# Expert layer kernel on one core: 102 up projections beside the gate matrix, and the sparse tile routed first

## The chip, the cores and the metric

The kernel runs on one core of a Trainium2 chip. The metric is the device time of one execution in microseconds; a version's time is the median of several runs. TensorE (PE in the rows), VectorE (DVE), ScalarE (ACT) and GpSimd (POOL) each run their own instruction queue in order; SyncE (SP) issues the plain DMAs, POOL the gathers.

## The reference, cut to what matters

512 tokens of width 1024 pass one layer: attention and convolution, an output projection, then a retrieval over 16384 single-neuron experts (PEER), then an embedding gate. The part that the change touches is the retrieval:

```
q = (mf @ wq).reshape(T, 8, 2, 128)
s = einsum('thcd,cnd->thcn', q, keys)              # 128 keys per half
sv, si = top_k(s, 16)
cand = sv[:, :, 0, :, None] + sv[:, :, 1, None, :]
cs, ci = top_k(cand.reshape(T, 8, 256), 16)
e1, e2 = si of half 0 and of half 1, picked by ci // 16 and ci % 16
experts = (e1 * 128 + e2).reshape(T, 128);  gates = softmax(cs)
a = einsum('cd,ckd->ck', x, u_tab[experts])
h = gelu(a) * gates
y = einsum('ck,ckd->cd', h, v_tab[experts])
```

Each token uses 128 of the 16384 experts. All data is float32.

## The kernel before

The retrieval is done in two ways. The first three token tiles (128 tokens each, NA = 3, TA = 384 tokens) are done **densely**: all 128 chunks c of 128 experts get an up projection (`up(c)`: expert rows by 384 tokens, then Gelu), the result is multiplied by a gate matrix that is zero where a token did not choose an expert, and a down projection (`down_prep(c)`, `down(c)`) adds up into six PSUM banks `y`. The fourth tile is done **sparsely**: `sparse(i)` gathers one expert row per token with an indirect DMA on POOL (256 gathers of 128 rows, first of u, then of v) and reduces it on DVE with one scalar_tensor_tensor (`scr` on L722 for u, `acc` on L730 for v). Four `row` buffers are in use in turn.

Every float32 product is made of three fp32r matmuls (`mm3`, L66 to L68): a weight tile `raw` is copied to a rounded `hi` on ACT and the rest `lo` is subtracted on DVE or POOL. So one up projection is 24 matmuls of 384 columns, one ACT copy (L583), one subtraction (`ulo`, L584) and one Gelu (L594, or L590 if the result goes to DRAM). One down chunk is 18 matmuls of 512 columns (L709).

The stages, in program order:

1. Front: attention, convolution, output projection, second norm. The change leaves it alone.
2. Routing, L596 to L616: 16 query projections of 24 matmuls (`qhi`, `qlo`), 16 times eight key matmul instructions (L611), and `top16` on DVE for each of 16 (head, half) scores of the three dense tiles. The scores of the sparse tile are copied to `sB` by ACT (L612). `pairs` then forms 112 candidate sums per head (L508, L510) and takes their top 16.
3. Gate matrix, L619 to L662: 12 up projections first; then per dense tile a `decodeA` (which expert, which gate) and 16 groups of GB = 8 tokens. A group builds one-hot rows in float16 on DVE (`o1v`, `eq`, and the two products L651 and L652; in every fourth group `o1a` comes from ACT instead of `o1v`), PE multiplies them (16 matmuls of 128 columns, L658) and ACT copies PSUM to `stage` (L660). A full stage (2 MB) goes to `g_spill` in DRAM. One up projection is emitted before every second group.
4. The up projections that are left of `first` (40 in all: chunks 0 to 23 are kept in SBUF, 16 more go to DRAM as `a_spill`), then `routeB` for the sparse tile (16 `top16`, `pairs`, `decode`, and `bidx`, the gather indices).
5. Experts, loop over c = 0 to 127: the up projection of chunk 24 + c or the load of a spilled one, the gate block `gt` for four chunks, the splits of the v tile, 18 down matmuls, and as many `sparse` steps as `sched(c)` asks for. Chunks from 104 on have no up projection.
6. Tail: gate and final norm, output.

The program is written in an order, but a planner at build time puts the instructions of each engine into their final order: it takes what is ready by priority, and up projections are seen to run well ahead of their place in the text. `keep_in_program_order` holds a single instruction back from that. Waits on buffers (two `uhi`, two `ulo`, three `uraw`, two PSUM banks `ups`, six `rbank`, two `stage`) set how far things can run ahead.

Of the kernel before, what the change touches and what calls it, by code (L numbers as in the profile page):

```python
# [10 lines left out]
F32 = mybir.dt.float32  # L11
# [17 lines left out]
NA = 3  # L29
TA = NA * 128  # L30
AHEAD = 24
SPILL = 16
GT = 32
NG = TA // GT
GB = 8
# [3 lines left out]
RATE, LATE = 1.38, 12  # L39
EVERY = 3  # L40
FIRST, STEP = 12, 2
# [12 lines left out]
def hymba_layer(ctx: ExitStack, tc: tile.TileContext, I, out):  # L54
# [38 lines left out]
    # ---------------------------------------------------------------- front  # L93
# [18 lines left out]
    # the tensor engine's clock comes up, and the first table, while the first loads are on their way  # L112
# [51 lines left out]
    # 1 / rms of every token, as a column per token tile and along the free axis of all partitions  # L164
# [78 lines left out]
    # attention in units of (head, query tile), three stages apart  # L243
# [65 lines left out]
    # the layer's own embedding, projected  # L309
# [51 lines left out]
    # the depthwise taps  # L361
# [5 lines left out]
    # conv layer norm + swish  # L367
# [18 lines left out]
    # ------------------------------------------------- output projection, second norm  # L386
    hd = tc.dram_tile([NT, 128, D], F32, name="h1_spill")
    ad = tc.dram_tile([SPILL, 128, TA], F32, name="a_spill")
# [73 lines left out]
    # ------------------------------------------------- expert routing  # L462
# [6 lines left out]
    gap = tc.alloc_tile_pool(name="gap", bufs=AHEAD, reuse_waits="tile")  # L469
# [12 lines left out]
    sB = rbp.tile([128, NH, 2, NK], F32, name="sB")  # L482
    jrep = rbp.tile([128, TOPK, 128], F16, name="jrep")
    A.activation(jrep, iota[:, 0:TOPK, None].to_broadcast([128, TOPK, 128]), AF.Copy)
    ne1 = rt.tile([128, NA, 128], F32, name="ne1")
# [5 lines left out]
    A.activation(irep, iota[:, :, None].to_broadcast([128, 128, 2]), AF.Copy)  # L491

# [8 lines left out]
    # of the sorted pairs (i, j) only those with (i + 1) * (j + 1) <= 16 can be among the first 16:  # L501
    # rows 0..3 whole and the first 4 of the others hold them all, in the order of their index
    NC0, NCAND = 4 * TOPK, 4 * TOPK + 12 * 4

    def pairs(st, t, h):
        sv, si, cs, ci = st
        cand = rbp.tile([128, NCAND], F32, name="cand", bufs=2)
        V.tensor_tensor(cand[:, 0:NC0].rearrange("p (a b) -> p a b", a=4), sv[:, t, h, 0, 0:4][:, :, None].to_broadcast([128, 4, TOPK]),  # L508
                        sv[:, t, h, 1][:, None, :].to_broadcast([128, 4, TOPK]), op=OP.add)
        V.tensor_tensor(cand[:, NC0:].rearrange("p (a b) -> p a b", a=12), sv[:, t, h, 0, 4:TOPK][:, :, None].to_broadcast([128, 12, 4]),  # L510
                        sv[:, t, h, 1, 0:4][:, None, :].to_broadcast([128, 12, 4]), op=OP.add)
        top16(cand, cs[:, t, h], ci[:, t, h], NCAND)
# [40 lines left out]
    def decodeA(t):  # L553
# [4 lines left out]
        A.activation(ne1[:, t], tp[:, 0:128], AF.Copy, scale=-1.0)  # L558
# [17 lines left out]
    first = list(range(AHEAD)) + list(spilled)  # L576

    def up(c):
# [5 lines left out]
        (P if c in first else V).tensor_tensor(lo, raw, f32(hi), op=OP.subtract)  # L584
# [11 lines left out]
    for h in range(NH):  # L596
        for c in range(2):
# [14 lines left out]
            A.activation(sB[:, h, c], sp[:, NA * 128:], AF.Copy)  # L612
            for t in range(NA):
                top16(sp[:, t * 128:t * 128 + 128], setA[0][:, t, h, c], setA[1][:, t, h, c], 128)
        for t in range(NA):
            pairs(setA, t, h)  # L616
    wqp.release()
    gst = tc.alloc_tile_pool(name="gst", bufs=2, reuse_waits="tile")
    for c in first[:FIRST]:  # L619
        up(c)  # L620
    nu = FIRST
    for t in range(NA):
        decodeA(t)
        for b in range(128 // GT):
            stage = gst.tile([128, NK, GT], F32, name="stage")
            for g in range(GT // GB):
                tk = b * GT + g * GB
                if g % STEP == 0 and nu < len(first):
                    up(first[nu])
                    nu += 1  # L630
# [6 lines left out]
                if g % ACT_EVERY == ACT_EVERY - 1:  # L637
                    ab = gst.tile([128, GB, 128], F16, name="ab", bufs=1)
                    for j in range(GB):
                        A.activation(ab[:, j], iota, AF.Abs, bias=ne1[:, t, tk + j:tk + j + 1])  # L640
                    o1 = gst.tile([128, GB, 128], F16, name="o1a", bufs=1)
                    A.activation(o1, ab, AF.Relu, bias=ones[:, 0:1], scale=-1.0)
                    pick1 = [o1[:, j] for j in range(GB)]
                else:
                    o1 = gst.tile(sh, F16, name="o1v")
                    V.tensor_tensor(o1, it, pairwise(e1T), op=OP.is_equal)
                    pick1 = [o1[:, j // 2, :, j % 2] for j in range(GB)]
# [22 lines left out]
    def ahead(c):  # L670
        if c in spilled:
# [241 lines left out]
```

## Time and profile before

| what | us |
|---|---|
| median of 3 runs | 1630.68 (1629.73 to 1630.71) |
| span of the profiled execution | 1628.7 |
| PE busy | 1538.4 (94%) |
| DVE busy | 1296.2 (80%) |
| ACT busy | 706.2 (43%) |
| POOL busy | 537.4 (33%) |

A PE row's duration contains the run through the array, and neighbouring matmuls overlap; so the cost of a matmul is read as the distance between the starts of matmuls that follow each other without a wait. A window of the trace lists the busy time of each engine, the granted TensorE clock as a share of 2.4 GHz, and the share of the DMA engines' time. The profiled execution's span is 2.0 us under the median of the runs.

### The profile page before, as it was taken

How to read it: one execution, taken by the hardware profiler on the slowest of the kernel's cores; microseconds unless marked ns; L12 is line 12 of the kernel's file. 1: busy time of each engine (PE TensorE's matmuls, PEld its weight loads, DVE VectorE, ACT ScalarE, POOL GpSimd, SP SyncE). 2: the span in 40 equal slices, each digit the busy share in tenths (PEclk: the TensorE clock that was granted, in tenths of full speed). 3: DMA queues.
4: the chain of work that ended last, by engine and by line, in shares of the span. 5: the costliest groups of instructions: out<-in, count | busy, mean ns of one | idle time of the engine just before them, and what ended most of it. 6: DMA issues, size and time to landing. Idle time of an engine off the chain costs nothing. (4 is left out here: it accounts for less than half of the span.)

```text
span 1628.7 us, 22295 instructions
## 1 busy us (share of the span) xinstructions
PE 1538.4 (94%) x7945; PEld 1334.0 (82%) x7945; DVE 1296.2 (80%) x2564; ACT 706.2 (43%) x1116; POOL 537.4 (33%) x360
## 2 busy tenths in 40 slices
PE   8999898999688887999999999999999999999997
PEld 6866576888577776988888889999999999997886
DVE  4999875988989998478887888777777777777657
ACT  5434643322488796433333333333333333324432
POOL 1000103442353342244444444444444444430000
PEclk9999998999899998999999999999999999999999
DMA  7210254221234645989999999988988899977612
GB/s 241 93 66 33 74 188 154 93 85 40 78 148 169 241 179 227 316 302 355 330 351 319 347 336 351 328 325 315 330 319 319 325 320 334 328 256 258 211 44 78
DMA packets 147648, 374.83 MB, mean 230 GB/s; under 512 B 12113, under 2 KB 66129, under 8 KB 146001
## 3 DMA queue, kind: packets, MB, share of 16 engines
q1 hardware_dynamic: 110672, 239.18, 42.3%
q0 software_dynamic: 36864, 134.23, 21.9%
q8 instruction: 62, 1.02, 0.2%
q14 instruction: 50, 0.40, 0.1%
HBM read 338.76 MB, written 34.60 MB: 229 GB/s over the span
## 5 line engine op out<-in xcount | busy, mean ns | idle before, releaser
L66 PE MATMUL ups<-mTH,uhi 128*128 128x384 f32 x1024 | 354.9, 347 | 4.0 <-ACT ga L594 4.0
L68 PE MATMUL ups<-mTH,ulo 128*128 128x384 f32 x1024 | 352.9, 345 | 5.6 <-POOL ulo L584 5.6
L67 PE MATMUL ups<-mTL,uhi 128*128 128x384 f32 x1024 | 351.2, 343 | 0.0
L583 ACT ACTIVATE uhi<-uraw 128x1024 fp32r<-128x1024 f32 x128 | 135.6, 1061 | 278.6 <-PE ups L67 251.5
L718 POOL DMA_INDIRECT row<-in_u,bidx x128 | 180.1, 1407 | 224.2 <-DVE scr L722 211.4
L718 POOL DMA_INDIRECT row<-in_v,bidx x128 | 182.6, 1427 | 206.8 <-DVE acc L730 189.4
L709 PE MATMUL y<-vlo,hH 128*128 128x512 f32 x768 | 238.5, 392 | 2.0 <-DVE vlo L63 2.0
L709 PE MATMUL y<-vhi,hH 128*128 128x512 f32 x768 | 239.0, 392 | 0.3 <-ACT vhi L62 0.3
L709 PE MATMUL y<-vhi,hL 128*128 128x512 f32 x768 | 239.0, 392 | 0.0
L66 PEld LDWEIGHTS ups<-mTH,uhi 128*128 128x128 f32 x1024 | 196.6, 192 | 8.6 <-ACT ga L594 4.6
L68 PEld LDWEIGHTS ups<-mTH,ulo 128*128 128x128 f32 x1024 | 196.1, 192 | 7.0 <-POOL ulo L584 6.9
L67 PEld LDWEIGHTS ups<-mTL,uhi 128*128 128x128 f32 x1024 | 196.0, 191 | 4.9
L62 ACT ACTIVATE hH<-hf 128x384 fp32r<-128x384 f32 x128 | 67.0, 524 | 285.2 <-issue 219.3
L63 DVE TENSOR_TENSOR hL<-hf,hH 128x384 fp32r<-128x384 f32 x128 | 71.2, 557 | 146.0 <-ACT hH L62 145.8
L584 POOL TENSOR_TENSOR ulo<-uraw,uhi 128x1024 fp32r<-128x1024 f32 x40 | 123.4, 3090 | 177.3 <-ACT uhi L583 155.6
L709 PEld LDWEIGHTS y<-vlo,hH 128*128 128x128 f32 x768 | 144.0, 188 | 35.4 <-DVE vlo L63 4.0
L709 PEld LDWEIGHTS y<-vhi,hL 128*128 128x128 f32 x768 | 144.2, 188 | 31.3 <-DVE rsq L73 0.2
L722 DVE SCALAR_TENSOR_TENSOR scr<-row,mB 128x1024 f32<-128x1024 f32 x128 | 156.1, 1220 | 15.4 <-DMA row<-in_u,bidx 15.4
L709 PEld LDWEIGHTS y<-vhi,hH 128*128 128x128 f32 x768 | 143.1, 188 | 25.4 <-ACT vhi L62 1.0
L730 DVE SCALAR_TENSOR_TENSOR acc<-row,bh,acc 128x1024 f32<-128x1024 f32 x127 | 162.5, 1279 | 0.0
L63 DVE TENSOR_TENSOR vlo<-vraw,vhi 128x1024 fp32r<-128x1024 f32 x128 | 156.1, 1220 | 0.8 <-ACT vhi L62 0.8
L584 DVE TENSOR_TENSOR ulo<-uraw,uhi 128x1024 fp32r<-128x1024 f32 x88 | 107.5, 1221 | 37.2 <-ACT uhi L583 37.1
(277 smaller groups left out, 2447.9 us busy)
## 6 DMA issues: line engine op xcount, KB each, us to landing
uraw<-in_ut SPq DMA_DIRECT2D x128, 512.0 KB, 6.1
vraw<-in_v SPq DMA_DIRECT2D x128, 512.0 KB, 4.7
g_spill<-stage SPq DMA_DIRECT2D x12, 2048.0 KB, 6.9
gt<-g_spill SPq DMA_DIRECT2D x32, 768.0 KB, 9.7
qraw<-in_wq SPq DMA_DIRECT2D x16, 512.0 KB, 3.6
wraw<-in_w_in SPq DMA_DIRECT2D x15, 512.0 KB, 3.9
woraw<-in_w_out SPq DMA_DIRECT2D x8, 512.0 KB, 4.2
et<-in_wg SPq DMA_DIRECT2D x8, 512.0 KB, 4.3
```

Source lines behind the costliest of these rows:

```text
L62: A.activation(hi, src, AF.Copy)
L63: V.tensor_tensor(lo, src, f32(hi), op=OP.subtract)
L66: T.matmul(ps, wh, xh, start=first, stop=False)
L67: T.matmul(ps, wh, xl, start=False, stop=False)
L68: T.matmul(ps, wl, xh, start=False, stop=last)
L583: A.activation(hi, raw, AF.Copy)
L584: (P if c in first else V).tensor_tensor(lo, raw, f32(hi), op=OP.subtract)
L709: T.matmul(y[t][n], w[:, sl], x[:, n * 512:n * 512 + 512], start=c == 0 and w is hH and x is hi, stop=c == NK - 1 and l)
L718: P.indirect_dma_start(out=row, out_offset=None, in_=I["u"] if i < 128 else I["v"], in_offset=bass.IndirectOffsetOnAxis(ap=bidx[:, j:j + 1 ...
L722: tc.keep_in_program_order(V.scalar_tensor_tensor(scr, row, 1.0, mB, op0=OP.mult, op1=OP.mult, accum_out=ba[:, j:j + 1]))
L730: tc.keep_in_program_order(V.scalar_tensor_tensor(acc, row, bh[:, j:j + 1], acc, op0=OP.mult, op1=OP.add))
```

## The change

- `AHEAD`, `SPILL` and the rest are replaced: 102 of 128 up projections (chunks 0 to 7, kept in SBUF, and 94 others that go to DRAM as `a_spill` and come back in the expert loop) are emitted in the routing and gate stages: 20 before the gate matrix, 4 after each `decodeA`, 3 before each group. The 26 chunks of `DIRECT` (11, 15, ..., 111) are done in the expert loop. The `lo` part of the first 20 is made on POOL, all others on DVE.
- The sparse tile is routed first: its `top16` reads PSUM (no `sB` copy), `routeB` is emitted ahead of the gate stage, and its u gathers are emitted there: two at three places per tile and ROWS = 4 per group, so 114 of the 128 in that stage. The other 14 and the 128 of v stay in the expert loop, spread by a new `sched`.
- `pairs` takes four heads at once (two additions for four heads instead of eight), and for the dense tiles it is emitted with the tile's decode.
- A group has GB = 16 tokens. Every third group's `o1` is made by a POOL subtraction and two ACT instructions over the whole group. The gate matmuls write PSUM with a step of four floats, so that the copy to `stage` reads in order and writes runs of four floats.
- `gt` is loaded for eight chunks at a time.

```
-AHEAD = 24
-SPILL = 16
+KEEP = 8
+DIRECT = [c for c in range(8, 112) if c % 4 == 3]
+GC = 8
-GB = 8
+GB = 16
+HG = 4
-RATE, LATE = 1.38, 12
-EVERY = 3
-FIRST, STEP = 12, 2
+FIRST, PER = 20, 3
+ROWS = 4
...
     def pairs(st, t, h):
         sv, si, cs, ci = st
-        cand = rbp.tile([128, NCAND], F32, name="cand", bufs=2)
...
+        hs = slice(h, h + HG)
+        cand = rbp.tile([128, HG, NCAND], F32, name="cand")
...
+        for j in range(HG):
+            top16(cand[:, j], cs[:, t, h + j], ci[:, t, h + j], NCAND)
...
     def routeB():
-        for h in range(NH):
-            for c in range(2):
-                top16(sB[:, h, c], setB[0][:, 0, h, c], setB[1][:, 0, h, c], 128)
-            pairs(setB, 0, h)
         ef = decode(setB, 0)
         V.tensor_copy(bgate, ef[:, 2])
-        V.scalar_tensor_tensor(ef[:, 0], ef[:, 0], float(NK), ef[:, 1], op0=OP.mult, op1=OP.add)
-        return ef[:, 0]
+        V.scalar_tensor_tensor(bidx, ef[:, 0], float(NK), ef[:, 1], op0=OP.mult, op1=OP.add)
...
-    spilled = {AHEAD + EVERY * i + EVERY - 1: i for i in range(SPILL)}
-    first = list(range(AHEAD)) + list(spilled)
+    spilled = {c: i for i, c in enumerate(c for c in range(KEEP, NK) if c not in DIRECT)}
+    first = list(range(KEEP)) + list(spilled)
+    EARLY = len(first)
...
-        (P if c in first else V).tensor_tensor(lo, raw, f32(hi), op=OP.subtract)
+        (P if c in first[:FIRST] else V).tensor_tensor(lo, raw, f32(hi), op=OP.subtract)
...
-            A.activation(sB[:, h, c], sp[:, NA * 128:], AF.Copy)
+            top16(sp[:, NA * 128:], setB[0][:, 0, h, c], setB[1][:, 0, h, c], 128)
             for t in range(NA):
                 top16(sp[:, t * 128:t * 128 + 128], setA[0][:, t, h, c], setA[1][:, t, h, c], 128)
-        for t in range(NA):
-            pairs(setA, t, h)
+        if h % HG == HG - 1:
+            pairs(setB, 0, h + 1 - HG)
...
-    for c in first[:FIRST]:
-        up(c)
-    nu = FIRST
+    nu, nxt = 0, 0
+
+    def more(n):
+        nonlocal nu
+        while n > 0 and nu < EARLY:
+            up(first[nu])
+            nu += 1
+            n -= 1
+
+    def rows(n):
+        nonlocal nxt
+        while n > 0 and nxt < 128:
+            sparse(nxt)
+            nxt += 1
+            n -= 1
+
+    routeB()
+    more(FIRST)
     for t in range(NA):
+        for h in range(0, NH, HG):
+            pairs(setA, t, h)
+            rows(2)
         decodeA(t)
+        rows(2)
+        more(4)
         for b in range(128 // GT):
             stage = gst.tile([128, NK, GT], F32, name="stage")
             for g in range(GT // GB):
                 tk = b * GT + g * GB
-                if g % STEP == 0 and nu < len(first):
-                    up(first[nu])
-                    nu += 1
+                more(PER)
+                rows(ROWS)
...
-                if g % ACT_EVERY == ACT_EVERY - 1:
-                    ab = gst.tile([128, GB, 128], F16, name="ab", bufs=1)
-                    for j in range(GB):
-                        A.activation(ab[:, j], iota, AF.Abs, bias=ne1[:, t, tk + j:tk + j + 1])
-                    o1 = gst.tile([128, GB, 128], F16, name="o1a", bufs=1)
-                    A.activation(o1, ab, AF.Relu, bias=ones[:, 0:1], scale=-1.0)
+                if (tk // GB + t * (128 // GB)) % ACT_EVERY == ACT_EVERY - 1:
+                    o1 = gst.tile([128, GB, 128], F16, name="o1", bufs=2)
+                    P.tensor_tensor(o1, iota16[:, None, :].to_broadcast([128, GB, 128]),
+                                    e1T[:, t, tk:tk + GB][:, :, None].to_broadcast([128, GB, 128]), op=OP.subtract)
+                    A.activation(o1, o1, AF.Abs)
+                    A.activation(o1, o1, AF.Relu, bias=ones[:, 0:1], scale=-1.0)
...
-                            T.matmul(gb[:, j * 128:j * 128 + 128], o2[:, i, jj // 2, :, jj % 2], pick1[jj], start=i == 0, stop=i == 1)
+                            T.matmul(gb[:, j::4], o2[:, i, jj // 2, :, jj % 2], pick1[jj], start=i == 0, stop=i == 1)
...
-                    A.activation(stage[:, :, t0:t0 + 4].rearrange("p e t -> p t e"),
-                                 gb.rearrange("p (t e) -> p t e", t=4), AF.Copy, scale=1.0 / GS)
+                    A.activation(stage[:, :, t0:t0 + 4], gb.rearrange("p (e t) -> p e t", t=4), AF.Copy, scale=1.0 / GS)
...
-    for c in first[nu:]:
-        up(c)
-    eB = routeB()
...
+    more(EARLY)
+    NU = NK - 24
+    nxt0 = nxt
+    def weight(c):
+        return c + 1 + sum(n <= c + KEEP for n in DIRECT)
     def sched(c):
-        return RATE * (c + 1 + sum(n not in spilled for n in range(AHEAD, AHEAD + min(c + 1, NU)))) - LATE
+        return nxt0 + (256 - nxt0) * weight(c) / weight(NU + 10)
...
     for c in range(NK):
-        if c < NU:
-            ahead(AHEAD + c)
+        if KEEP + c in DIRECT:
+            up(KEEP + c)
+        elif KEEP + c < NK:
+            ga[KEEP + c] = gap.tile([128, TA], F32, name="ga")
+            load(ga[KEEP + c], ad[spilled[KEEP + c]])
         parts = down_prep(c)
```

## Rows read from the trace of the kernel before

**Rows 1.** The page's 40 slices of the span: busy tenths of PE and DVE.
```profile
PE   8999898999688887999999999999999999999997
...
DVE  4999875988989998478887888777777777777657
```

**Rows 2.** Windows: stretch, its length; busy us of each engine, clock, DMA share, GB/s.
```profile
264.00:410.00 146.00, 144.91 (x733) 124.51 (x731) 119.59 (x688) 46.49 (x72) 56.54 (x24) 0.99 0.24 81
410.00:450.00 40.00, 25.96 (x135) 23.98 (x136) 39.58 (x81) 17.65 (x35) 13.70 (x6) 0.83 0.23 79
450.00:646.00 196.00, 157.35 (x1293) 144.34 (x1292) 186.33 (x371) 161.19 (x246) 81.52 (x23) 0.91 0.50 192
646.00:669.00 23.00, 23.00 (x123) 23.00 (x121) 6.83 (x12) 10.06 (x14) 7.06 (x4) 0.91 0.71 260
264.00:669.00 405.00, 351.22 (x2277) 315.83 (x2276) 352.33 (x1149) 235.40 (x364) 158.83 (x56) 0.93 0.39 145
...
669.00:1470.00 801.00, 801.00 (x3978) 722.95 (x3977) 625.79 (x788) 283.61 (x386) 360.49 (x254) 1.00 0.91 327
```

**Rows 3.** Tile hH: count, ns min/median/max, first and last start, us.
```profile
L709 PE MATMUL y<-vhi,hH x768: 387/389/628, 669.1 to 1570.1; 128*128 128x512 f32 x192
```

**Rows 4.** Timeline of PE from 494.7: start us, us, what, count.
```profile
494.71 0.34 PE L67 MATMUL ups<-mTL,uhi 128*128 128x384 f32 x1
...
496.62 2.01 PE L658 MATMUL rbank<-o1v,o 128*128 128x128 f16 x32
498.44 0.42 PE L66 MATMUL ups<-mTH,uhi 128*128 128x384 f32 x1
```

**Rows 5.** Timeline of PE among down projections, two matmuls a row.
```profile
1477.54 0.62 PE L709 MATMUL y<-vhi,hH 128*128 128x512 f32 x2
...
1482.07 0.62 PE L709 MATMUL y<-vlo,hH 128*128 128x512 f32 x2
```

**Rows 6.** Timeline of PE, the key matmuls of one query projection.
```profile
273.20 1.16 PE L611 MATMUL rbank<-keysT,qT 128*128 128x128 f32 x8
```

**Rows 7.** Groups by line: count, busy us, mean ns, idle before and releaser.
```profile
L718 POOL DMA_INDIRECT row<-in_u,bidx x128 | 180.1, 1407 | 224.2 <-DVE scr L722 211.4 <-DMA vraw<-in_v 6.3 <-DVE ulo L584 2.9
...
L722 DVE SCALAR_TENSOR_TENSOR scr<-row,mB 128x1024 f32<-128x1024 f32 x128 | 156.1, 1220 | 15.4 <-DMA row<-in_u,bidx 15.4
...
L583 ACT ACTIVATE uhi<-uraw 128x1024 fp32r<-128x1024 f32 x128 | 135.6, 1061 | 278.6 <-PE ups L67 251.5 <-POOL ulo L584 11.7 <-issue 8.9
...
L584 DVE TENSOR_TENSOR ulo<-uraw,uhi 128x1024 fp32r<-128x1024 f32 x88 | 107.5, 1221 | 37.2 <-ACT uhi L583 37.1
...
L651 DVE TENSOR_TENSOR o<-eq,gTH 128x1024 f16<-128x1024 f16 x48 | 44.8, 933 | 2.2 <-PE rbank L658 2.2
...
L652 DVE TENSOR_TENSOR o<-eq,gTL 128x1024 f16<-128x1024 f16 x48 | 39.3, 819 | 0.0
...
L510 DVE TENSOR_TENSOR cand<-sv 128x48 f32<-128x48 f32 x32 | 22.1, 692 | 0.0
...
L722 DVE DVE_READ_ACCUMULATOR scr<-row,mB 128x1 f32 x128 | 10.6, 83 | 0.0
```

**Rows 8.** Single lines: ns min/median/max, first and last start.
```profile
L651 DVE TENSOR_TENSOR o<-eq,gTH x48: 667/682/2872, 443.6 to 643.1; 128x1024 f16<-128x1024 f16 x48
...
L584 POOL TENSOR_TENSOR ulo<-uraw,uhi x40: 2351/2460/9224, 267.4 to 657.6; 128x1024 fp32r<-128x1024 f32 x40
```

**Rows 9.** Waits from 410 to 650: who for whom, us, times, longest.
```profile
PEld L658 <- DVE o L651: 41.6, 21, 10.1
```

**Rows 10.** Timeline of SP after the last gate group.
```profile
647.44 0.32 SPq L59 DMA_DIRECT2D g_spill<-stage  x1
...
658.42 0.37 SPq L59 DMA_DIRECT2D gt<-g_spill  x1
```

**Rows 11.** Tile row: time of its transfers from issue to landing.
```profile
DMA to landing us min/median/max: 2.0/7.2/11.7
```

**Rows 12.** Waits of SP's queue over the span: us, times, longest.
```profile
SPq L59 <- DVE hf L701: 36.6, 25, 5.2
```

More of the change, by code (lines that the diff above doesn't have):

```diff
@@ L491, in hymba_layer @@
     A.activation(irep, iota[:, :, None].to_broadcast([128, 128, 2]), AF.Copy)
+    iota16 = rt.tile([128, 128], F16, name="iota16")
+    A.activation(iota16, iota, AF.Copy)
     def top16(src, vals, idx, n):
@@ L564, in routeB, with new_row, sparse @@
     def routeB():
-        for h in range(NH):
-            for c in range(2):
-                top16(sB[:, h, c], setB[0][:, 0, h, c], setB[1][:, 0, h, c], 128)
-            pairs(setB, 0, h)
         ef = decode(setB, 0)
         V.tensor_copy(bgate, ef[:, 2])
-        V.scalar_tensor_tensor(ef[:, 0], ef[:, 0], float(NK), ef[:, 1], op0=OP.mult, op1=OP.add)
-        return ef[:, 0]
+        V.scalar_tensor_tensor(bidx, ef[:, 0], float(NK), ef[:, 1], op0=OP.mult, op1=OP.add)
+    def new_row():
+        return gp.tile([128, D], F32, name="row", bufs=4)
+    def sparse(i):
+        j = i % 128
+        row = new_row()
+        P.indirect_dma_start(out=row, out_offset=None, in_=I["u"] if i < 128 else I["v"],
+                             in_offset=bass.IndirectOffsetOnAxis(ap=bidx[:, j:j + 1], axis=0))
+        if i < 128:
+            scr = gp.tile([128, D], F32, name="scr")
+            tc.keep_in_program_order(V.scalar_tensor_tensor(scr, row, 1.0, mB, op0=OP.mult, op1=OP.mult, accum_out=ba[:, j:j + 1]))
+            if j % 32 == 31:
+                js = slice(j - 31, j + 1)
+                A.activation(bh[:, js], ba[:, js], AF.Gelu)
+                V.tensor_tensor(bh[:, js], bh[:, js], bgate[:, js], op=OP.mult)
+        elif j == 0:
+            V.tensor_scalar(acc, row, bh[:, 0:1], None, op0=OP.mult)
+        else:
+            tc.keep_in_program_order(V.scalar_tensor_tensor(acc, row, bh[:, j:j + 1], acc, op0=OP.mult, op1=OP.add))
     ga = {}
-    spilled = {AHEAD + EVERY * i + EVERY - 1: i for i in range(SPILL)}
-    first = list(range(AHEAD)) + list(spilled)
+    spilled = {c: i for i, c in enumerate(c for c in range(KEEP, NK) if c not in DIRECT)}
+    first = list(range(KEEP)) + list(spilled)
+    EARLY = len(first)
     def up(c):
@@ L668, in hymba_layer @@
     psy = tc.alloc_tile_pool(name="psy", bufs=1, space=PSUM, reuse_waits="tile")
-    def ahead(c):
-        if c in spilled:
-            ga[c] = gap.tile([128, TA], F32, name="ga")
-            load(ga[c], ad[spilled[c]])
-        else:
-            up(c)
-    for c in first[nu:]:
-        up(c)
-    eB = routeB()
-    gp = tc.alloc_tile_pool(name="gp", bufs=1, reuse_waits="tile")
     ex = tc.alloc_tile_pool(name="ex", bufs=2, reuse_waits="tile")
@@ L710, in down @@
                          stop=c == NK - 1 and l)
-    def new_row():
-        return gp.tile([128, D], F32, name="row", bufs=4)
-    def sparse(i):
-        j = i % 128
-        row = new_row()
-        P.indirect_dma_start(out=row, out_offset=None, in_=I["u"] if i < 128 else I["v"],
-                             in_offset=bass.IndirectOffsetOnAxis(ap=bidx[:, j:j + 1], axis=0))
-        if i < 128:
-            scr = gp.tile([128, D], F32, name="scr")
-            tc.keep_in_program_order(V.scalar_tensor_tensor(scr, row, 1.0, mB, op0=OP.mult, op1=OP.mult, accum_out=ba[:, j:j + 1]))
-            if j % 32 == 31:
-                js = slice(j - 31, j + 1)
-                A.activation(bh[:, js], ba[:, js], AF.Gelu)
-                V.tensor_tensor(bh[:, js], bh[:, js], bgate[:, js], op=OP.mult)
-        elif j == 0:
-            V.tensor_scalar(acc, row, bh[:, 0:1], None, op0=OP.mult)
-        else:
-            tc.keep_in_program_order(V.scalar_tensor_tensor(acc, row, bh[:, j:j + 1], acc, op0=OP.mult, op1=OP.add))
     def ple(t, h2, pool, pbank):
```

37 lines of the change are left out of this document (15 added, 22 removed).

## The prediction

> **What bounds the kernel now.** I read the 40 slices first: PE is full but for the slices from 400 to 650 us (and the front, which the change leaves alone) [rows 1]. The windows of that part come next: from 264, where the query projections start, to the first down projection at 669 [rows 3], PE is busy 351 us of 405 and its granted clock averages 0.93; in 450 to 646, the gate groups, it is 157 of 196 at 0.91, while DVE is busy 186 [rows 2]. What ends PE's idle time there is DVE: the weight loads of the gate matmuls wait 41.6 us for one DVE line alone [rows 9]. From 669 to 1470 PE is busy throughout at full clock, DVE 626 of 801, the DMA engines 0.91 [rows 2]. So the kernel is bound by PE everywhere but in routing and gate matrix, where DVE holds it up. PE work put there is worth what PE loses there.
>
> What PE loses is counted from distances between starts. An up matmul: (496.62 - 494.71) / 11 = 0.1736 us, so an up projection is 24 of them, 4.17 us. The 32 gate matmuls: 498.44 - 496.62 = 1.82, 0.057 each [rows 4]. A down matmul: 4.53 / 20 = 0.2265, a chunk of 18 is 4.08 [rows 5]; a query matmul has the same 512 columns. The keys take 1.16 per projection [rows 6]. Before the first down projection there are 16 x 24 x 0.2265 = 87, keys 16 x 1.16 = 19, 40 ups 167, 768 gate matmuls 44: 316 us of work in 405, so **89 us are lost**. Afterwards 88 ups (367) and 128 chunks (522) are 889 us; the stage from 669.1 to 1570.1 takes 901 [rows 3], so 12 us (1.4%) are lost. The rest behind it, 58.6 us, stays.
>
> **The change part by part.** *PE.* 62 up projections (258 us) move from the expert loop ahead of it. The early stage then holds 87 + 19 + 102 x 4.17 (425) + 44 = 575 us of PE work, the loop 26 x 4.17 + 522 = 630. With no waits at all the gates would end at 264 + 575 = 839 and the span at 839 + 630 + 9 + 58.6 = 1537. That is the far end of the gain, 92 us; all else is what is lost again.
>
> *DVE in the early stage.* Busy now 352 us of the 405 [rows 2]. Added: 80 more `ulo` on DVE at 1.22, 98 us; 114 u rows at 1.22 and 0.08 for the accumulator read, 148 us [rows 7]. Taken away: the additions of `pairs`, of which L510 alone has 22 us at 692 ns for 48 elements [rows 7]; 16 instructions over four heads at some 0.3 each remain, so about -20. A third of the groups rather than a quarter has its `o1` elsewhere, about -10. The four float16 lines do the same elements in half as many instructions; L651 takes 682 ns in the median but 933 in the mean, with a longest of 2872, against 819 in L652 (L650 lies between) [rows 7, 8]. The long ones lie where POOL runs a subtraction. 20 of POOL's 40 `ulo` go, eight `o1` of twice the size come: -40 if all collisions went, 0 if the new ones cost as much; I take -20. Sum: 352 + 98 + 148 - 20 - 10 - 20 = 548, between 525 and 575. So DVE gets nearly as full as PE, and the earlier remedy (DVE off the path) is not to be had.
>
> *ACT and SP.* ACT is busy 235 of 405 [rows 2]; 62 more ups bring 62 x (1.06 + about 0.5 for Gelu) = 97 [rows 7], the sixteen `sB` copies go, the stage copies cost as much or less, the eight `o1` replace the old ones: some 330 of 600, not a bound. SP gets 78 more stores of 192 KB and as many loads. The loads wait for `hf` to free one of eight `ga` buffers, and v and `gt` loads queue behind them; who would wait is ACT's split of v. SP waits for `hf` already 25 times, longest 5.2 us [rows 12], in the loop in which PE loses 1.4% in all, so I cost this at nothing; if the cover goes, 94 waits of 1 us are the price of a few per cent of the loop.
>
> *The expert loop.* Up to c = 103 it takes 104 x 4.08 + 26 x 4.17 = 533 us. In it move 104 v tiles and 26 u tiles of 512 KB, the `gt` blocks, 94 spilled blocks and about 132 gathers of 512 KB, some 176 MB: 330 GB/s, against 327 now at a DMA share of 0.91 [rows 2]. DVE there: 104 x 2.2 + 26 x 1.2 + 132 x 1.3 = 430 of 533, 0.80 as now (626 / 801). The loop keeps its ratios, so I keep its loss of 1.4%: 639 us.
>
> *The losses that stay in the early stage.* At each dense tile DVE must do pairs and decode before the next group's one-hots exist. The stretch 410 to 450 is one such: DVE 39.6 of 40, PE 26.0 at a clock of 0.83 [rows 2], 14 us of idle and some 4 of slow clock. The first of three now lies under the 20 ups in front; the second and third have four ups (17 us) but as much more DVE work (four `ulo`, six rows). I take 18 each, 36, and 9 for the start and for groups in which a row is late: 45. Gates end at 264 + 575 + 45 = 884. (DVE: 548 of 620, 0.88, against 352 of 405, 0.87, now.)
>
> *The boundary.* Now the last `stage` store is issued at 647.4, the first `gt` load at 658.4, the first down matmul at 669.1 [rows 10, 3], and PE is busy all the 23 us from 646 to 669 [rows 2], because four spilled ups are left over and one more follows. The change's counts (20 + 3 x 4 + 24 x 3 = 104) leave none; only the ups of chunks 11 and 15 could be drawn forward, 8 us in two PSUM banks. `gt` is twice as large. So 22 us less 8: I take 14, between 0 and 25. First down at 898.
>
> **Sum:** 898 + 639 + 58.6 = 1595.6 against the span of 1628.7; the runs' median lies 2.0 above that span, so 1597.
>
> **The PSUM step.** No matmul here writes PSUM with a step. The nearest row is the key matmul, which for 128 float32 columns takes 1.16 / 8 = 0.145 us against the gate's 0.057 [rows 6, 4]; that bounds the cost by 768 x 0.088 = 68 us, and below by nothing, since the same columns go through the array. I take 0. The Trainium skill, "PSUM — Partial Sum Buffer", section Specifications, speaks against it: 8-byte cachelines, and "any non-contiguous AP slows matmuls significantly". No run here shows it so far; it gives no figure, and is the page beside the second rival.
>
> **The rivals.** *First, slower: rows late on DVE.* A gather takes 1.41 on POOL [rows 7] and lands 7.2 later, at most 11.7 [rows 11]; four buffers used in one burst come back after 4 x 1.41 + 7.2 = 12.8 us. A group lasts 3 x 4.17 + 1.8 = 14.3 on PE, so 1.5 are to spare. But every third group POOL also makes an `o1` of 2048 elements; 1024 took 2.35 alone, up to 9.2 beside DVE [rows 8], so 4.7 to 18. If it stands ahead of the gathers and takes 9.4, eight groups are late by 8 us, +63: 1660. DVE takes its queue in order, so `ulo` (the ups) and `o2` (the gate matmuls) wait behind the row. It decides from about 6 us per `o1`: then 8 x 4.5 = 36 brings it to the time before. Against it: `o1` needs only decoded indices, and POOL idles 224 us around the u gathers now [rows 7], so it can be made early. Chance 0.15.
> *Second: stepped PSUM writes slow the gate matmuls* up to the key row's 0.145: +68, of which the waits for DVE absorb a third: 1642. Against it: nothing in the trace. Chance 0.10.
> *Third: better.* The planner starts pairs and decodes of the next tile among the groups, as it moves ups now, and two ups cover most of the boundary: 10 + 6 instead of 45 + 14: 1554. For it: in 264 to 410 ups keep PE at 145 of 146 [rows 2]. Chance 0.15.
> *Fourth: it does less than it says.* Ups wait for `ulo` on a full DVE, fall behind and run after the gates; the boundary is covered, the gate stage loses as now, 89: about 1628. Chance 0.05.
>
> **How the numbers follow.** My forecast, 1570 to 1622, has 0.55: 1597. Range: from 1554 of the third rival to 1648, above the second; the first is left out in its upper part. What can be told from no change here is about 0.2%, 3 us. Faster: 0.55 + 0.15 and about 0.06 from mild forms of the rivals, 0.76; within 0.2%: 0.06; slower: the first and most of the second, 0.18.
>
> **What would show it.** In the new trace: first down near 898, last near 1537. PE 575 us of work between 264 and 884, with two holes of some 18 us at the decodes and one of 14 before the first down. 32 gate matmuls still in 1.8 us (the PSUM step). DVE's wait for `row` small (rival one). L651 near 1.2 us for 2048 elements, with few long ones. The loop at 0.91 of DMA share and full clock. I am wrong if DVE waits for rows by tens of us, if gate matmuls stretch, if the loop loses over 3%, or if the holes aren't there.

## The result, and the profile after

The changed kernel takes 1692.23 us (1689.7 to 1693.58) against 1630.2 for the kernel before on the same chip: 1.038 times, interval 1.0365 to 1.0401. It is 62 us slower, and the forecast of 1597 and its range are both missed on the slow side.

The down projections first, in the view of tile hH (its row of all 768 matmuls: ns min/median/max, first and last start), after [rows 3]:

```profile
L735 PE MATMUL y<-vhi,hH x768: 387/389/793, 987.7 to 1632.0; 128*128 128x512 f32 x192
```

The loop takes 1632.0 - 987.7 = 644 us, 5 more than the 639 of the forecast, and 59 follow it (58.6). Most of the miss is ahead of it: the first down matmul comes at 987.7 where 898 was forecast. The windows of that stage (columns as in [rows 2]):

```profile
264.00:410.00 146.00, 145.05 (x730) 124.86 (x731) 97.65 (x597) 41.31 (x53) 54.77 (x23) 0.98 0.26 85
410.00:518.00 108.00, 85.73 (x442) 83.01 (x441) 106.98 (x273) 33.50 (x48) 42.81 (x24) 0.87 0.53 171
518.00:962.00 444.00, 416.24 (x2575) 407.99 (x2574) 345.82 (x445) 196.90 (x275) 184.55 (x112) 0.96 0.83 299
962.00:988.00 26.00, 9.23 (x54) 8.91 (x52) 8.11 (x13) 5.17 (x8) 2.61 (x2) 0.72 0.90 314
264.00:988.00 724.00, 656.26 (x3794) 624.78 (x3795) 558.57 (x1325) 276.88 (x382) 284.74 (x160) 0.94 0.67 237
988.00:1500.00 512.00, 506.66 (x2325) 432.68 (x2325) 390.67 (x463) 183.75 (x246) 210.81 (x126) 0.99 0.89 320
```

The stage has 724 us instead of 898 - 264 = 634. DVE's busy time, 559, is within the forecast (548, between 525 and 575), and ACT's 277 is under the 330 allowed. So neither of these two sums was wrong by much. PE is idle in three places (410 to 518, scattered through the gate groups, and in the 26 us before the first down matmul), and in between it is busy with something that takes longer than before. That something is in PE's timeline (start, length, what) [rows 4]:

```profile
611.22 0.34 PE L69 MATMUL ups<-mTH,ulo 128*128 128x384 f32 x1
611.40 3.67 PE L699 MATMUL rbank<-o,o 128*128 128x128 f16 x32
614.82 0.42 PE L67 MATMUL ups<-mTH,uhi 128*128 128x384 f32 x1
```

32 gate matmuls now take 614.82 - 611.40 = 3.42 us, 0.107 each, where they took 1.82 and 0.057. Over 768 matmuls this is 768 x 0.050 = 38 us of PE work that was not in the sum.

The idle within the groups shows in a stretch of the timeline with one of the eight groups whose `o1` is begun on POOL (L680) and finished on ACT (L682, L683); L605 makes `uhi`, L612 is the Gelu of an up projection:

```profile
576.78 4.64 POOL L680 TENSOR_TENSOR o<-iota,e1T 128x2048 f16<-128x2048 f16 x1 [0.43 <-PE rbank L699]
...
581.46 1.91 ACT L682 ACTIVATE o<-o 128x2048 f16<-128x2048 f16 x1 [4.12 <-POOL o L680]
...
583.40 2.00 ACT L683 ACTIVATE o<-o,ones 128x2048 f16<-128x2048 f16 x1
...
585.31 0.47 ACT L612 ACTIVATE av<-ups 128x384 f32<-128x384 f32 x1
585.68 1.99 ACT L605 ACTIVATE uhi<-uraw 128x1024 fp32r<-128x1024 f32 x2
...
586.78 0.45 PE L67 MATMUL ups<-mTH,uhi 128*128 128x384 f32 x1 [1.76 <-ACT uhi L605]
...
588.61 0.69 PE L69 MATMUL ups<-mTH,ulo 128*128 128x384 f32 x1 [1.21 <-DVE ulo L606]
```

ACT has nothing to do for 4.12 us, because the instruction at the head of its queue waits for POOL, and then 3.9 us of `o1` work stand before the `uhi` that PE needs next. PE stops twice. In the waits of 264 to 990 this is one row (who for whom: us, times, longest); the second row is the last place, before the first down matmul:

```profile
ACT o L682 <- POOL o L680: 38.3, 8, 7.2
...
PE y L735 <- ACT vhi L63: 16.8, 1, 16.8
```

And 410 to 518 has its longest stop here. L553 is the Exp at the end of a decode. It runs four times, first for the sparse tile; the one below is the third, so it belongs to the second dense tile. The first dense tile's Exp had run at 446.95, and its decoded indices (`e1T`) reach SBUF only behind the Exp below, so the planner has drawn the next tile's pairs and decode ahead of the first tile's gate groups (the first gate matmul starts at 518.3):

```profile
476.45 0.31 ACT L553 ACTIVATE gts<-gts 128x128 f32<-128x128 f32 x1 [12.86 <-DVE gts L552]
...
478.46 1.99 ACT L605 ACTIVATE uhi<-uraw 128x1024 fp32r<-128x1024 f32 x2
...
479.56 0.69 PE L67 MATMUL ups<-mTH,uhi 128*128 128x384 f32 x1 [10.13 <-ACT uhi L605]
...
481.25 0.28 ACT L565 ACTIVATE e1T<-rbank 128x128 f16<-128x128 f32 x1 [0.41 <-PE rbank L564]
```

It is the same form: ACT stands at an instruction whose input DVE has not made, with the next `uhi` behind it.

### The profile page after: what moved, and what is told of

The parts are those of the page before. It is cut to its first block, busy times and chain, and to the rows that moved or that the text cites. A ratio compares the mean times of both kernels' runs of the same rounds, so it can differ in the third digit from the quotient of the medians.

```text
span 1690.9 us, 22356 instructions
## 1 busy us (share of the span) xinstructions
PE 1576.0 (93%) x7945; PEld 1375.6 (81%) x7945; DVE 1294.8 (77%) x2443; ACT 656.8 (39%) x1006; POOL 534.0 (32%) x348
## 5 line engine op out<-in xcount | busy, mean ns | idle before, releaser
L69 PE MATMUL ups<-mTH,ulo 128*128 128x384 f32 x1024 | 355.9, 348 | 26.7 <-DVE ulo L606 17.2
L67 PE MATMUL ups<-mTH,uhi 128*128 128x384 f32 x1024 | 356.5, 348 | 23.4 <-ACT uhi L605 21.0
L581 POOL DMA_INDIRECT row<-in_v,bidx x128 | 217.2, 1697 | 315.3 <-DVE acc L593 304.6
L605 ACT ACTIVATE uhi<-uraw 128x1024 fp32r<-128x1024 f32 x128 | 134.5, 1058 | 322.1 <-PE ups L68 277.8
L67 PEld LDWEIGHTS ups<-mTH,uhi 128*128 128x128 f32 x1024 | 200.2, 195 | 27.8 <-ACT uhi L605 23.5
L606 DVE TENSOR_TENSOR ulo<-uraw,uhi 128x1024 fp32r<-128x1024 f32 x108 | 132.1, 1223 | 87.7 <-ACT uhi L605 82.0
L585 DVE SCALAR_TENSOR_TENSOR scr<-row,mB 128x1024 f32<-128x1024 f32 x128 | 161.3, 1260 | 20.9 <-DMA row<-in_u,bidx 19.7
L63 ACT ACTIVATE vhi<-vraw 128x1024 fp32r<-128x1024 f32 x128 | 135.7, 1060 | 16.6 <-DMA vraw<-in_v 16.5
```

Source lines behind the costliest of these rows:

```text
L63: A.activation(hi, src, AF.Copy)
L67: T.matmul(ps, wh, xh, start=first, stop=False)
L69: T.matmul(ps, wl, xh, start=False, stop=last)
L581: P.indirect_dma_start(out=row, out_offset=None, in_=I["u"] if i < 128 else I["v"], in_offset=bass.IndirectOffsetOnAxis(ap=bidx[:, j:j + 1 ...
L585: tc.keep_in_program_order(V.scalar_tensor_tensor(scr, row, 1.0, mB, op0=OP.mult, op1=OP.mult, accum_out=ba[:, j:j + 1]))
L605: A.activation(hi, raw, AF.Copy)
```

## The experiments

Theory: four things that the sum left out or priced too low make the 95 us between the forecast and the measured time: the PSUM step, `o1` on POOL and ACT, the stretch before the first gate group, the boundary. Rival: rows late on DVE, as the first rival of the prediction had it. The times are medians; the ratio to the kernel before on the same chip is formed from all runs and can differ by 0.1% from the quotient of the medians:

| run | edit | us | ratio (95%) |
|---|---|---|---|
| e1_nostep | changed kernel, no PSUM step, old copy | 1662.7 | 1.0204 (1.0162 to 1.0246) |
| e2_o1dve | changed kernel, every `o1` on DVE | 1660.3 | 1.0179 (1.0152 to 1.0206) |
| e2b_o1buf3 | changed kernel, three `o1` buffers | 1689.3 | 1.0361 (1.0316 to 1.0406) |
| e3_before_step | kernel before, with step and new copy | 1622.4 | 0.9953 (0.9938 to 0.9968) |
| e9_before_read | kernel before, new copy without step | 1631.9 | 0.9997 (0.9980 to 1.0013) |
| e6_step2 | changed kernel, step of two floats | 1695.4 | 1.0387 (1.0367 to 1.0407) |
| e7_norows | changed kernel, all gathers in the loop | 1748.9 | 1.0743 (1.0710 to 1.0777) |
| e8_exp_first | changed kernel, Exp at the start of decode | 1692.8 | 1.0394 (1.0366 to 1.0422) |
| e4_read | no step, short copy, `o1` on DVE | 1634.5 | 1.0031 (1.0011 to 1.0051) |
| e5_left | e4_read, seven ups behind the last group | 1636.7 | 1.0041 (1.0030 to 1.0053) |
| e11_lessrows | e4_read, six rows fewer at the first decode | 1629.3 | 1.0000 (0.9984 to 1.0016) |
| e10_ulodve | e4_read, the first 20 `ulo` on DVE | 1617.6 | 0.9929 (0.9910 to 0.9947) |

**e1_nostep: the PSUM step.**

```
-T.matmul(gb[:, j::4], ...)
+T.matmul(gb[:, j * 128:j * 128 + 128], ...)
-A.activation(stage[:, :, t0:t0 + 4], gb.rearrange("p (e t) -> p e t", t=4), ...)
+A.activation(stage[:, :, t0:t0 + 4].rearrange("p e t -> p t e"),
+             gb.rearrange("p (t e) -> p t e", t=4), ...)
```

> The changed kernel with the gate matmuls writing PSUM without a step, and the copy to the stage strided as in the kernel before. Theory A (the step doubles the gate matmul): 32 gate matmuls in about 1.85 us instead of 3.67, and since PE ends the gate groups, about -39 us: 1653. Rival B (DVE or late rows end the groups, the step is hidden): the 32 in 1.85 us all the same, but the time falls by under 10 us. The stage copy goes back from 0.60 to about 1.1 us; I expect no cost from it, ACT being half idle.

It comes out 30 us faster. The gate matmuls' row is back at the old length (310 ns in the median with the step):

```profile
L699 PE MATMUL rbank<-o,o x768: 218/218/235, 514.6 to 926.8; 128*128 128x128 f16 x192
```

The last gate matmul comes at 926.8 and the first down matmul at 954.0 instead of 987.7, 34 us earlier. So nearly all of the 38 us of PE work was on the path, although the copy went back to 1181 ns in the mean from 595.

**e2_o1dve and e2b_o1buf3: the `o1` by POOL and ACT.**

```
-if (tk // GB + t * (128 // GB)) % ACT_EVERY == ACT_EVERY - 1:
+if False:
```

> The changed kernel with every o1 made on DVE, none on POOL and ACT. Theory C (the eight o1 groups stall PE because ACT stands in its queue for POOL's subtraction and then 4 us for Abs and Relu, with the copies for the next up projections behind it; some 5 us each with the slow clock after it): about -35 to -45 us, 1652, and PE full in 540 to 962. Rival B (DVE ends the groups): eight more DVE lines of 1.14 us make it 9 us slower, 1701.

```
-o1 = gst.tile(..., name="o1", bufs=2)
+o1 = gst.tile(..., name="o1", bufs=3)
```

> The changed kernel with three buffers for o1 instead of two, nothing else. If the stall comes from POOL starting late (its subtraction waits for the gate matmuls that free a buffer), an earlier start takes ACT's 38 us of waiting away: -25 to -40 us, about 1660. If ACT's own 4 us of Abs and Relu in front of the up copies are enough for the stall, only -5 to -10: 1684.

With every `o1` on DVE the kernel is 32 us faster, though DVE got eight instructions of 1.2 us more; between 518 and 900 PE is then busy 370 of 382 (357 in the changed kernel). The stretch from 518 to the last gate matmul is 30 us shorter, 414 for 444. Of these, 16 are waits of PE: those for `uhi` go from 10.5 to nothing, those for DVE's `ulo` from 17.2 to 11.6. The other 14 are busy time of PE for the same work, at a granted clock of 0.98 instead of 0.96. A third buffer (for `o1` of either kind) gives 3 us, within the intervals. It lets POOL begin earlier, but ACT's row of waits for POOL is hardly shorter, 35.8 us in 7 where it was 38.3 in 8. So the buffer isn't what costs. That `o1` on POOL and ACT costs 32 us is shown by the run. That it costs them through ACT's queue, where two instructions that depend on POOL stand before the copies that feed PE, is read from the waits for `uhi`. No run kept POOL's subtraction and took only ACT's part away, and POOL's subtraction has another effect that goes with it. It stretches a DVE instruction beside it, as the gate product `o` shows, in the changed kernel (first line) and in e2_o1dve:

```profile
L693 DVE TENSOR_TENSOR o<-eq,gTL 128x2048 f16<-128x2048 f16 x24 | 49.7, 2070 | 0.0
...
L693 DVE TENSOR_TENSOR o<-eq,gTL 128x2048 f16<-128x2048 f16 x24 | 29.2, 1218 | 0.0
```

These are 20 us of DVE's time, in a stretch where DVE is busy 346 of 444 us. Part of the 32 us can come from there.

**e3_before_step and e9_before_read: the step in the kernel before.** The first puts the step and the new copy into the kernel before (the edit of e1_nostep the other way round). The second keeps the matmuls as they were and only lets the copy read PSUM with a step and write runs of four:

```
-A.activation(stage[:, :, t0:t0 + 4].rearrange("p e t -> p t e"),
-             gb.rearrange("p (t e) -> p t e", t=4), ...)
+A.activation(stage[:, :, t0:t0 + 4], gb.rearrange("p (t e) -> p e t", t=4), ...)
```

> The kernel before with the stepped PSUM write and the short stage copy alone. Theory A: 16 gate matmuls in about 1.8 us instead of 1.0, 39 us more PE work in a stage where PE waits for DVE 40 us anyway: between +5 and +39, I take +15, 1645. If the step costs only where PE ends the stage, nearer to 0; the stage copy at 0.6 instead of 1.1 us gives nothing.

> The kernel before, with nothing changed but the copy to stage, which reads PSUM with a step of 128 floats and writes runs of four. With a stepped write and the short copy it took 1622.4. If it is the short copy that pays there, through ACT, the same gain comes without the step: 1620 to 1623. If the step cost something there too, it is faster still, down to 1612.

Both expectations fail. With the step the kernel before is 0.5% faster, not slower; with the short copy alone nothing changes. The copy takes 597 ns in one and 599 in the other, so what differs is the step, and the order in which the copy reads PSUM, which doesn't change its length. Their windows of the gate groups, e3_before_step first (before: [rows 2], 157 busy at 0.91):

```profile
450.00:646.00 196.00, 186.17 (x1325) 176.86 (x1324) 187.01 (x375) 130.66 (x253) 75.01 (x23) 0.98 0.53 194
```

and e9_before_read:

```profile
450.00:646.00 196.00, 160.70 (x1290) 148.05 (x1289) 181.66 (x368) 124.77 (x251) 81.16 (x23) 0.89 0.50 188
```

There DVE ends the groups. The longer matmuls fill time in which PE waited (its wait for `o` is 19.6 us with the step, 42.2 without), so they cost nothing, and the clock granted in that stretch is 0.98 instead of 0.89. The mean clock of the whole execution says the same in every run: 0.982 to 0.987 in the ten with the step, at most 0.977 in those of e9_before_read. That the higher clock is where the 8 us come from was not tried by itself. What is shown: the same step costs 30 us where PE is full, and nothing where it waits.

**e6_step2: a shorter step.**

```
-T.matmul(gb[:, j::4], ...)
+T.matmul(gb.rearrange("p (a e b) -> p a e b", a=2, b=2)[:, j // 2, :, j % 2], ...)
...
```

> The changed kernel, but its gate matmuls write PSUM with a step of two floats (8 bytes) instead of four (16), with the copy adapted. If the cost goes with the distance (0.107 us at four, 0.057 at one), it is some 0.07 to 0.08 a matmul and the time between 1663 and 1692, about 1672. If any step costs the full price, 0.107 and 1692.

The copy is adapted to it. A step of two floats costs what a step of four costs: 310 ns in the median and 32 matmuls in 3.67 us by the same row, and no measurable difference in time. The Trainium skill, "PSUM — Partial Sum Buffer", section Specifications, gives 8-byte cachelines and says that a non-contiguous pattern slows matmuls significantly. The trace agrees and puts a size to it: 0.107 us against 0.057, at a step of two floats (8 bytes) as at four.

**e7_norows: the rows as a cause.**

```
-ROWS = 4
+ROWS = 0
...
-            rows(2)
...
-        rows(2)
```

> The changed kernel with no u gathers in the gate stage; all 256 stay in the expert loop, where the schedule spreads them (from none done, instead of from 114). Rival B (rows late on DVE): the gate stage shortens by tens of us. Theories A and C (the step, and ACT's queue): the early stage ends at the same time within 15 us, since DVE idles there anyway (346 of 444 us busy from 518 to 962), and the loop, with 1.9 instead of 1.05 gathers per unit of work on a DMA share of 0.9, gets slower by tens of us: 1692 to 1750.

All 128 u gathers go to the expert loop. The first down matmul comes at 962.5, 25 us earlier, but the loop takes 725 us instead of 644, at a DMA share of 0.96 and 358 GB/s: 57 us slower in all. So the gathers stand well where the change put them, and taking them away doesn't win the time back. They aren't free there: 25 us is more than the 15 that theories A and C allowed. How much of it is their work on DVE and how much is waiting isn't shown. In the changed kernel DVE waits 19.7 us for u rows, 3.8 at the longest, where the rival had 63 us in eight late groups. As the main cause it falls.

**e8_exp_first: the Exp of the decode.** The subtraction and the Exp (L552, L553) go to the beginning of `decode`.

> The changed kernel with the subtraction and the Exp of the decode moved from its end to its beginning, nothing else. Theory D (from 410 to 490 ACT stands in its queue for DVE's subtraction before the Exp, once 12.9 us, with the copies for the next up projections behind it; PE waits 10 us for one of them and then runs at the low clock): -10 to -20 us, 1677, and PE's wait at about 479 gone. If the wait comes from DVE's subtraction for the up (ulo) instead, under 5 us.

Nothing changes. ACT still waits 13.1 us for the subtraction and PE 9.2 for `uhi`. The subtraction runs right behind the last `top16` of that tile's pairs in both (at 474.4, and 476.2 in the changed kernel), so the place in the text was not the cause.

**e4_read: both causes out, and the copy kept short.**

```
-if (tk // GB + t * (128 // GB)) % ACT_EVERY == ACT_EVERY - 1:
+if False:
...
-T.matmul(gb[:, j::4], ...)
+T.matmul(gb[:, j * 128:j * 128 + 128], ...)
-A.activation(stage[:, :, t0:t0 + 4], gb.rearrange("p (e t) -> p e t", t=4), ...)
+A.activation(stage[:, :, t0:t0 + 4], gb.rearrange("p (t e) -> p e t", t=4), ...)
```

> Both cures at once: gate matmuls without a step and every o1 on DVE; but the copy to the stage now reads PSUM with a step of 128 floats and writes runs of four. If A and C add up (-30 and -32 measured singly): 1630, between 1622 and 1640. The copy: 0.60 us if what made it short was the runs in its output, 1.1 if it was the plain order of its input.

The two effects add up: 58 us off, nearly all of the 62 by which the changed kernel is slower than the one before. The copy takes 606 ns in the mean although it now reads PSUM with a step of 128 floats, so it is the runs of four that it writes which make it short, not the order in which it reads. The first down matmul is at 931.1, 33 us later than forecast: the last gate matmul starts at 904.0 where the gates were to end at 884, and 27.1 us follow it where 14 were forecast. The longest loss of PE ahead of the boundary is the stretch 410 to 500.

**e5_left: the boundary.** With Exp first as in e8_exp_first and

```
-more(PER)
+more(PER if nu < EARLY - 7 else 0)
```

> The kernel with both cures, the Exp first, and seven of the 102 up projections held back until after the last gate group, where the changed kernel has PE idle for 17 us before the first down projection (the last stage goes to DRAM and comes back as the first gate block). Expected: both cures 1630, less 10 to 15 for the Exp, less 12 to 18 for the boundary: 1603. If the boundary is bound by something else (the v split), only 1615.

Seven ups are left to cover the way of the last `stage` through DRAM. The first down matmul comes at 920.3, 11 us earlier, and PE's wait there falls from 18.4 to 2.6. Yet the loop takes 655.6 us (649.7 in e4_read, 645.6 in e10_ulodve), and the time is the same as without. The trace shows where most of the gain goes. Ahead of the first down matmul 816 L67 matmuls run, eight to an up projection, where e4_read has 832: two ups of the loop had been drawn into the boundary, and now they are done in the loop, 8 us. And the gate matmuls, with fewer ups between them, wait 8.0 us for `o`, where they waited nothing. Work moved into the gap left a gap where it had been.

**e10_ulodve and e11_lessrows: the stretch before the first gate group.** In e10_ulodve nothing but the engine of the first 20 `ulo` changes; in e11_lessrows the six rows emitted with the first tile's pairs and decode stay for the loop.

```
-(P if c in first[:FIRST] else V).tensor_tensor(lo, raw, f32(hi), op=OP.subtract)
+V.tensor_tensor(lo, raw, f32(hi), op=OP.subtract)
```

> The version without the PSUM step and with all o1 on DVE (1634.5), and now the first 20 ulo on DVE too. What is open is the loss of some 34 us around the first decode (410 to 500 us), where DVE is busy 89.5 of 90. Theory A, DVE's instructions are stretched by POOL's subtractions beside them (2.4 to 3.8 us where 1.2 is the rule): without these POOL work some 20 us of DVE time come back, 20 ulo of 1.22 are added, some 9 of them after 410; the loss falls to 20 or 25 and the time to some 1625. Theory B, DVE simply has too much work there: nine ulo more, 11 us, the loss grows to some 45 and the time to 1645.

```
     for h in range(0, NH, HG):
         pairs(setA, t, h)
-        rows(2)
+        rows(2 if t else 0)
     decodeA(t)
-    rows(2)
+    rows(2 if t else 0)
```

> The same version (1634.5), with the six u rows that are emitted beside the first tile's pairs and decode left for the expert loop. They take 9.8 us of DVE in 410 to 500. Theory B (DVE's work before the first gate group is the bound): the loss of 34 falls by 8 to 10, the loop gains six rows (0.7 us each by the run with all rows in the loop, 4 us): some 1629. Rival, the stretch is bound by ACT's place in its queue and POOL's ulo, not by the amount of work on DVE: PE's loss there stays at 34, the loop is 4 us longer: 1638.

Giving DVE 20 subtractions more makes the kernel 17 us faster and beats the kernel before by 0.7%. The windows 410 to 500, e4_read:

```profile
410.00:500.00 90.00, 69.84 (x339) 66.93 (x338) 89.47 (x239) 28.07 (x40) 38.86 (x21) 0.85 0.53 169
```

and e10_ulodve:

```profile
410.00:500.00 90.00, 85.20 (x482) 83.63 (x482) 88.95 (x261) 35.48 (x49) 14.12 (x11) 0.98 0.62 211
```

DVE is full in both, but in the second it does 261 instructions instead of 239, 16 `ulo` more among them, in the same time. The timeline of e4_read shows what is different:

```profile
421.61 2.40 POOL L606 TENSOR_TENSOR ulo<-uraw,uhi 128x1024 fp32r<-128x1024 f32 x1 [4.40 <-ACT uhi L605]
421.64 2.66 DVE L557 TENSOR_TENSOR ef<-gts,gs 128x128 f32<-128x128 f32 x1
...
430.20 2.95 DVE L525 CAST s<-si 128x256 f16<-128x256 uint32 x1
...
430.55 2.36 POOL L606 TENSOR_TENSOR ulo<-uraw,uhi 128x1024 fp32r<-128x1024 f32 x1
...
441.62 2.39 POOL L606 TENSOR_TENSOR ulo<-uraw,uhi 128x1024 fp32r<-128x1024 f32 x1
442.08 0.27 DVE L500 MAX8 cs<-cand 128x8 f32<-128x112 f32 x1
```

The first two DVE instructions end 0.2 to 0.3 us behind the POOL subtraction that they meet, so they do their own work when it is over. Not every DVE instruction is held up: the ones of `top16` that run beside the third subtraction keep their 0.27 us. The means by line (count | busy us, mean ns), in e4_read:

```profile
L547 DVE TENSOR_TENSOR eq<-eq,s 128x2048 f16<-128x2048 f16 x5 | 10.4, 2077 | 0.0
...
L538 DVE CAST dc<-iu 128x128 f32<-128x128 uint32 x3 | 5.1, 1692 | 0.0
...
L557 DVE TENSOR_TENSOR ef<-gts,gs 128x128 f32<-128x128 f32 x2 | 3.1, 1526 | 0.0
```

and in e10_ulodve, without POOL subtractions beside them:

```profile
L547 DVE TENSOR_TENSOR eq<-eq,s 128x2048 f16<-128x2048 f16 x5 | 6.1, 1219 | 0.0
...
L557 DVE TENSOR_TENSOR ef<-gts,gs 128x128 f32<-128x128 f32 x2 | 0.8, 396 | 0.0
L538 DVE CAST dc<-iu 128x128 f32<-128x128 uint32 x3 | 0.8, 264 | 0.0
```

The Trainium skill, "SBUF — State Buffer", section "SBUF: two separate sides", says that GpSimd and a DVE instruction that reads two inputs from SBUF, or runs in a two-port mode, share a pair of ports as an exclusive lock: the one that starts first has it for its whole instruction, and the other blocks. The trace agrees: a cast of 0.26 us is 1.69 in the mean, and the subtraction of 2.40 us above cost DVE 2.66 - 0.40 = 2.3, while DVE needs 1.22 to do it itself. ACT's longest wait for `gts` goes from 12.0 us to 1.9, and PE's for `uhi` (9.4) is gone. Gone too are 8.1 us in which PE waited for POOL's `ulo` itself, which takes 2.4 us there and 1.22 on DVE. So the run shows that the `ulo` on POOL cost 17 us; how much of that was DVE held up, and how much POOL's own slowness, it doesn't separate.

Taking six rows off DVE instead leaves PE's busy time there where it was (69.1 of 90), and ACT's wait even grows (14.3), as the rival to theory B expected. Its time, 1629.3, is what theory B gave, but its interval (0.9984 to 1.0016) touches that of e4_read (1.0011 to 1.0051), so the gain can be noise, and it does not come from this stretch. What e10_ulodve shows holds without it: POOL's work beside the decode cost the stretch, more than the amount of DVE's.

## Why the prediction was wrong, point by point

**What bounds the kernel, and the method.** Right in the main: the tail keeps its 59, and the up projections cost PE about the same in either place. Without the three costs below, in e10_ulodve, the last gate matmul starts at 885.5 where 884 was forecast. That it fits so closely is luck in part, because the 45 us of loss lie elsewhere. The third rival's premise came true: the planner ran all four decodes early (in e10_ulodve the last Exp starts at 598.0, in the changed kernel at 562.7). So the two holes of 18 us in which the groups were to wait for the second and third decode aren't there: no gate matmul waits for `o` in e10_ulodve. Instead PE loses 24.2 us in nine waits for `ulo` on DVE.

**The PSUM step, taken at 0.** This step failed, and it was the one with a row at its upper bound: 0.145 for the key matmul and 0 below. The matmul measured 0.107, and 38 of the 68 us. "The same columns go through the array" is no reason for a lower end of nothing; what the prediction itself named against the change, though without a figure, should have moved the value toward the row. The row was also misread. The prediction takes the cost of a matmul from the distance between starts, but the 1.16 of [rows 6] is a length; the next matmul starts 0.92 after the keys:

```profile
274.12 0.48 PE L66 MATMUL rbank<-mTH,qhi 128*128 128x512 f32 x1
```

That is 0.115 a matmul, an upper bound of 45 us, and nearer to what came. On the path the step cost 30 us (e1_nostep). The second rival had the right mechanism, and with these 30 us the forecast would have been 1627, no gain to speak of. It got a chance of 0.10.

**ACT, "some 330 of 600, not a bound".** The sum was right (277 of 724), the conclusion wrong. This step of the prediction failed: it didn't ask what is queued behind the new instruction on its engine. The prediction saw POOL's `o1` only as something that delays gathers (first rival); it delays ACT, and through ACT `uhi`. With what it takes from DVE that is 32 us (e2_o1dve).

**DVE, 548 of 620.** The sum was right again. "The first of three now lies under the 20 ups in front" was not: those ups have their `ulo` on POOL, which stretches the very decodes that they were to cover, and their `uhi` stands behind the Exp of the next tile's decode. I counted POOL's collisions in the float16 lines (-20 for the `ulo` that go), but not where the other 20 would lie. It cost 17 us (e10_ulodve against e4_read).

**The boundary, 14.** In e10_ulodve 27.3 us pass from the last gate matmul (885.5) to the first down matmul (912.8); two ups run in them, as forecast, and PE waits 18.6. The 22 us had been counted from the issue of the last store. From there they hold in the changed kernel too, 987.7 - 965.7:

```profile
965.28 0.33 SPq L60 DMA_DIRECT2D uraw<-in_ut  x1
965.71 0.38 SPq L60 DMA_DIRECT2D g_spill<-stage  x1
...
978.08 0.37 SPq L60 DMA_DIRECT2D gt<-g_spill  x1
```

But that store is issued 3.5 us after the start of the last gate matmul (962.2), 5.0 in e10_ulodve, and that piece was left out. The last copy to `stage` was over at 963.1. The store stood in SP's queue behind the load of a u tile, which had to wait until a `ulo` (964.0 to 965.2) freed its buffer. It is the same form as on ACT, in another queue. The doubled `gt` block isn't it: from its issue to the first down matmul 987.7 - 978.1 = 9.6 us pass, before it was 10.7 [rows 10, 3].

**The loop, 639, and SP's loads, "at nothing".** The loop does not keep its loss of 1.4%. Before the first down matmul 104 up projections have run, 102 and the two in the boundary, so the loop's work is 24 x 4.17 + 522 = 622 us, and the 644 hold 22 us of loss, 3.5%. The kernel before has 41 and 87 by the same count, not 40 and 88, and loses 16, 1.8%. What is new is the wait that the prediction named and costed at nothing: ACT's split of v waits for its load, in the kernel before (first line) and after:

```profile
L62 ACT ACTIVATE vhi<-vraw 128x1024 fp32r<-128x1024 f32 x128 | 135.5, 1058 | 0.5 <-ACT hH L62 0.4
...
L63 ACT ACTIVATE vhi<-vraw 128x1024 fp32r<-128x1024 f32 x128 | 135.7, 1060 | 16.6 <-DMA vraw<-in_v 16.5
```

Behind the first down matmul PE waits 10.6 us for `vhi` and `vlo`, 2.3 in the kernel before. No run was made on it, so whether the 94 loads more on SP are the reason is open.

**The sum again.** From 1692.2 to the 1617.6 of e10_ulodve 75 us go with the three costs. The rest, 20 us, is the boundary and the loop. The prediction let the two ups drawn forward shorten the boundary by 8 us and left them in the loop's work as well. That doesn't change its sum, but its parts are then 906 for the first down matmul and 631 for the loop. e10_ulodve has 912.8 and 645.6, so some 7 us are left at the first down matmul and 15 in the loop. Profiled executions of this loop differ (639.3 in e11_lessrows, 649.7 in e4_read), but all lie above 631.

**The rivals.** The first, rows late on DVE, fell as the main cause (e7_norows). The second happened in part. The third's premise came true without its gain. The range ended at 1648 because slow cases were taken one at a time. Three came together (30, 32 and 17 us), and only the first of them, the PSUM step, stood among the rivals.

## What to carry to other kernels

Before moving work onto an engine that is half idle, read what is queued behind it on that engine: an instruction that waits holds back everything after it, and a sum of busy time doesn't show that. POOL is not a free helper beside DVE: a subtraction there can take from DVE nearly its own length (2.3 of 2.40 us here). And a cost that is hidden in one stage, as the PSUM step was under DVE, comes out in full when the change fills the engine that hid it.

## What the runs showed of the hardware that I had not expected

- A gate matmul of 128 float16 columns takes 0.057 us to contiguous PSUM and 0.107 to PSUM with a step of two or of four floats.
- An ACT copy of 128x512 from PSUM takes 1181 ns in the mean if each written run is one float, and 606 if it is four, though the 606 reads PSUM with a step of 128 floats.
- In the kernel before, the longer matmuls went with a shorter time (0.9953), with a granted clock of 0.98 in the gate groups where the short copy without the step had 0.89.
- A DVE instruction of 0.40 us that met a POOL subtraction took 2.66; MAX8 beside such a subtraction kept its 0.27.
